# A 3x3 convolution on one core: the first output pair stored by halves, fewer loads issued ahead, idle matmuls four times as wide

## The chip, the cores and the metric

The kernel runs on one core of a Trainium2 chip. The core has TensorE (matrix products, its weight loads shown apart), VectorE, ScalarE, GpSimd and SyncE, each with an instruction queue of its own, and 16 DMA engines that all queues share. The metric is the device time of one execution in microseconds. The profile's span runs from the first to the last instruction; the time is a little longer.

## The reference

The input is 16 images of 64 channels, 64 by 64 pixels, in f32; the weight is 128 x 64 x 3 x 3, of which about nine in ten values are zero (the kernel does not use that). The output is 16 images of 128 channels:

```python
x_pad = np.pad(x, ((0, 0), (0, 0), (pad, pad), (pad, pad)), mode='constant')
for b in range(batch):
    for co in range(c_out):
        for ci in range(c_in):
            for kh in range(k):
                for kw in range(k):
                    if weight[co, ci, kh, kw] != 0:
                        output[b, co] += weight[co, ci, kh, kw] * x_pad[b, ci, kh:kh+h, kw:kw+w]
```

So 16.8 MB of input and 0.29 MB of weight are read, and 33.6 MB of output are written.

## The kernel before

Two images make a pair: 2 x 64 channels fill the 128 partitions, and there are eight pairs, 0 to 7. A pair's input is kept in a bf16 tile of its own, `xs[p]`; the f32 to bf16 conversion is done by the load itself, issued from GpSimd (`load`, L68). Only the first 32 rows of pair 0, the head, come as f32 through SyncE (L62), into the first buffer of the `o` pool, and are cast on VectorE and ScalarE (`cast_x`, L99). The `o` pool has seven buffers of one f32 output image each, so pair p uses two, and the buffers come round again after three pairs.

Every pair is worked off in four blocks of 16 rows, numbered here 0 to 31 through the whole kernel. Block 0 is computed directly (`direct`): nine taps per 8 rows and image. All others go through `twos`: GpSimd adds neighbouring rows (`s`, L167, in three buffers), TensorE makes one product of that sum for both output rows (copied out by ScalarE to `pc`, L174), then two products for the even and the odd rows (L148), and VectorE adds `pc` while it takes each out of PSUM (L181, four per block: even rows of image 0 and 1, then odd rows of image 0 and 1).

The order of each queue is the order of the program; nothing is rescheduled. SyncE issues the weight, the head, and then all stores: of pairs 0 to 6 one 2 MB store per image when the pair is done (L207), of pair 7 two of 1 MB per image, after its second and fourth block (L204). GpSimd issues the other half of pair 0 (L63), then pairs 1, 2 and 3 whole and 24 rows of pair 4 (L68). The other 40 rows of pair 4 are issued behind the sum of pair 1's last block, and pair p + 3 behind the sum of pair p's last block, for p = 2, 3, 4.

At the start, before any input is there, TensorE runs 27 matmuls on a tile of zeros (`keep_busy`, L84), which VectorE has cleared (L79); then nine that transpose the weights (L109); then 28 more on zeros. The first real matmul follows, and waits for the head's cast.

Of the kernel before, what the change touches and what calls it, by code (L numbers as in the profile page):

```python
# [8 lines left out]
FP32 = mybir.dt.float32  # L9
BF16 = mybir.dt.bfloat16  # L10
# [17 lines left out]
def kernel(  # L28
# [6 lines left out]
    nc = tc.nc  # L35

    B, C_IN, H, W = x.shape
    C_OUT, _, KH, KW = weight.shape
    assert (B, C_IN, H, W) == (16, 64, 64, 64) and (C_OUT, KH, KW) == (128, 3, 3)
    NP = B // 2  # L40
    HEAD = 32

    const_pool = ctx.enter_context(tc.tile_pool(name="const", bufs=1))
# [4 lines left out]
    psum_pool = ctx.enter_context(  # L48
        tc.tile_pool(name="psum", bufs=8, space=bass.MemoryType.PSUM)
    )  # L50
# [4 lines left out]
    def pair(p):  # L55
        return x[2 * p : 2 * p + 2].rearrange("n i h w -> (n i) h w")

    xs = [x_pool.tile([128, H, W], BF16, name=f"x{p}") for p in range(NP)]
# [5 lines left out]
    ident = const_pool.tile([128, 128], BF16, name="ident")  # L64
    make_identity(nc, ident)

    def load(p, a=0, b=H):
        nc.gpsimd.dma_start(out=xs[p][:, a:b, :], in_=pair(p)[:, a:b, :])  # L68

    EARLY, CUT = 4, 24
    for p in range(1, EARLY):
        load(p)
    load(EARLY, 0, CUT)


    idle_rhs = const_pool.tile([128, 128], BF16, name="idle_rhs")
    nc.vector.memset(idle_rhs, 0.0)  # L79
    idle_ps = psum_pool.tile([128, 128], FP32, name="ps")  # L80

    def keep_busy(n):
        for _ in range(n):
            nc.tensor.matmul(idle_ps, idle_rhs, idle_rhs, start=True, stop=True)  # L84

    keep_busy(27)

# [8 lines left out]
    def cast_x(copy, a, b):  # L98
        copy(out=xs[0][:, a:b, :], in_=x_head[:, a:b, :])  # L99
# [24 lines left out]
    nc.vector.tensor_copy(out=wT[:, G0], in_=ps0)  # L124
    ps2 = transposed(G2)
    nc.scalar.copy(out=wT[:, G2], in_=ps2)
    keep_busy(28)
    cast_x(nc.scalar.copy, 9, 18)
    difference(G01, ps0)
    difference(G21, ps2)  # L130
# [26 lines left out]
    def direct(p, o, r0, rows):  # L157
        ps = product(
            [(xs[p], G1, r0, 1), (xs[p], G0, r0 - 1, 1), (xs[p], G2, r0 + 1, 1)], rows
        )  # L160
        nc.scalar.copy(out=o[0][:, r0 : r0 + rows, :], in_=ps[0])  # L161
        nc.vector.tensor_copy(out=o[1][:, r0 : r0 + rows, :], in_=ps[1])  # L162

    def twos(p, o, r0):
        t0 = r0 // 2
        s = s_pool.tile([128, 8, W], BF16, name="s")
        nc.gpsimd.tensor_tensor(  # L167
            out=s, in0=xs[p][:, r0 : r0 + 16 : 2, :], in1=xs[p][:, r0 + 1 : r0 + 16 : 2, :], op=ADD
        )
        shared = product([(s, G1, 0, 1)], 8)  # L170
        pc = []
        for n in range(2):
            c = p_pool.tile([128, 8, W], FP32, name="pc")
            nc.scalar.copy(out=c, in_=shared[n])  # L174
            pc.append(c)
        even = [(xs[p], G21, r0 + 1, 2), (xs[p], G0, r0 - 1, 2)]
        odd = [(xs[p], G01, r0, 2), (xs[p], G2, r0 + 2, 2)]
        for first, terms in ((r0, even), (r0 + 1, odd)):
            ps = product(terms, 8)
            for n in range(2):  # L180
                nc.vector.tensor_tensor(  # L181
                    out=o[n][:, first : r0 + 16 : 2, :], in0=ps[n], in1=pc[n], op=ADD
                )

    for p in range(NP):
        o = [o_pool.tile([C_OUT, H, W], FP32, name="o") for _ in range(2)]
        last = p == NP - 1
        for blk in range(4):
            r0 = 16 * blk
            if BLOCKS[p][blk] == "T":  # L190
                twos(p, o, r0)


                if p == 1 and blk == 3:
                    load(EARLY, CUT, H)
                elif p > 1 and blk == 3 and p + EARLY - 1 < NP:
                    load(p + EARLY - 1)
            else:
                for r, rows in ((r0, 8), (r0 + 8, 8)):
                    direct(p, o, r, rows)  # L200
            if last and blk % 2 == 1:
                for n in range(2):
                    rows = slice(r0 - 16, r0 + 16)
                    nc.sync.dma_start(out=out[2 * p + n][:, rows, :], in_=o[n][:, rows, :])  # L204
        if not last:
            for n in range(2):
                nc.sync.dma_start(out=out[2 * p + n], in_=o[n])  # L207

# [29 lines left out]
```

## Time and profile before

| what | value |
|---|---|
| four runs, us | 126.51, 126.59, 131.04, 131.05 |
| their median, us | 128.81 |
| the profiled execution: time, us | 126.51 |
| its span, us | 124.7 |
| mean granted TensorE clock | 0.957 |
| busy share: TensorE, VectorE, GpSimd, ScalarE | 87%, 66%, 33%, 31% |
| matmuls of the computation (L148) | 966, from 7.23 us to about 110.3 us |
| VectorE's combinations (L181) | 124 of 686 ns |
| GpSimd's row sums (L167) | 31 of 1151 ns |
| loads with conversion (L68): issue to landing | 11.9 to 24.4 us |
| stores of 2 MB (L207): issue to landing | 10.3 to 25.6 us |
| stores of 1 MB (L204): issue to landing | 9.9 to 13.3 us |

Busy times are of one execution. In the lines on stretches of time the columns are: the stretch, its length, then busy time and number of instructions of TensorE, its weight loads, VectorE, ScalarE and GpSimd, then the granted TensorE clock, the DMA engines' share, and the GB/s that landed. In the lines of the timeline they are: start, length, engine, line of the kernel, operation, what is written from what, number of instructions, and in brackets the idle time before and what ended it. A DMA's landing is counted from its issue, so it holds the time that it stood behind other transfers.

### The profile page before, as it was taken

The page shows a single profiled execution, that of the slowest core. Times are in us where ns is not written, and L with a number is a line of the kernel's source. Part 1 is how long each engine was busy: PE and PEld are TensorE (multiplying, and loading weights), DVE is VectorE, ACT ScalarE, POOL GpSimd, SP SyncE. Part 2 cuts the span into 40 slices and gives each one's busy share as a digit, 9 for nine tenths or more (in the row PEclk, how much of TensorE's full clock was granted, in tenths as well). Part 3 has the DMA queues.
Part 4 walks back from the last instruction along what each step waited for, and adds up shares of the span by engine and source line. Part 5 has one row for each costly group of instructions (what it writes and reads, how often), then busy time and mean ns, then how long its engine had stood idle before and what let it go on. Part 6 is the DMA issues. An engine that isn't in the chain of part 4 may idle for free.

```text
span 124.7 us, 2543 instructions
## 1 busy us (share of the span) xinstructions
PE 108.9 (87%) x1030; PEld 59.8 (48%) x1030; DVE 82.3 (66%) x135; ACT 39.0 (31%) x71; POOL 41.1 (33%) x46
## 2 busy tenths in 40 slices
PE   6989999999999999999999999999999999940000
PEld 6845555555555555555555555555555555510000
DVE  0364777877787778777877787778777878870000
ACT  4555323333333333333333333333333333300000
POOL 6437343533353335333533333333333300000000
PEclk9999999999999999999999999999999999997555
DMA  4999999999999999999999999999999999999991
GB/s 134 345 227 215 213 215 213 203 386 334 339 428 410 310 297 331 439 305 331 313 433 315 299 334 418 420 439 420 436 436 420 431 426 426 431 407 420 428 389 50
DMA packets 4188, 42.93 MB, mean 344 GB/s; under 512 B 464, under 2 KB 464, under 8 KB 976
## 3 DMA queue, kind: packets, MB, share of 16 engines
q1 hardware_dynamic: 2880, 34.90, 66.6%
q0 software_dynamic: 1296, 7.86, 30.8%
q8 instruction: 8, 0.13, 0.4%
q14 instruction: 4, 0.03, 0.1%
HBM read 17.07 MB, written 33.55 MB: 406 GB/s over the span
## 4 chain that ended last, share of the span: by engine, by line
PE 82%; DMA 4%; DVE 1%; issue 1%; DVEq 0%; SPq 0%
PE ps L148 82%; DMA o<-in_x_dram 4%; DVE o L181 1%; DVEq L233 0%; DVE x L99 0%; SPq L60 0%; DVEq L181 0%
## 5 line engine op out<-in xcount | busy, mean ns | idle before, releaser
L181 DVE TENSOR_TENSOR o<-ps,pc 128x512 f32<-128x512 f32 x124 | 77.8, 686 | 22.1 <-PE ps L148 19.8
L148 PE MATMUL ps<-x,wT 64*128 64x504 bf16 (+3 forms) x780 | 88.8, 373 | 0.5 <-DVE x L99 0.5
L148 PEld LDWEIGHTS <-wT 64*128 64x128 bf16 x966 | 54.8, 94 | 48.8 <-issue 0.5
L167 POOL TENSOR_TENSOR s<-x 128x512 bf16<-128x512 bf16 x31 | 35.6, 1151 | 57.4 <-PE ps L148 43.2
L174 ACT COPY pc<-ps 128x512 f32<-128x512 f32 x62 | 33.3, 589 | 64.0 <-issue 61.8
L148 PE MATMUL ps<-s,wT 64*128 64x512 bf16 (+1 forms) x186 | 25.7, 377 | 0.0
L84 PE MATMUL ps<-idle_rhs 128*128 128x128 bf16 x55 | 4.8, 265 | 1.0 <-DVE idle_rhs L79 1.0
L84 PEld LDWEIGHTS <-idle_rhs 128*128 128x128 bf16 x55 | 4.4, 122 | 1.0 <-DVE idle_rhs L79 1.0
L68 POOL DMA_DIRECT2D x<-in_x_dram x8 | 4.4, 561 | 0.0
L103 DVE CAST w_bf<-w_sb 128x192 bf16<-128x192 f32 (+1 forms) x4 | 1.1, 360 | 2.6 <-DMA w_sb<-in_weight_dram 2.6
L162 DVE COPY o<-ps 128x512 f32<-128x512 f32 x2 | 1.4, 692 | 2.0 <-PE ps L148 2.0
L161 ACT COPY o<-ps 128x512 f32<-128x512 f32 x2 | 1.2, 586 | 2.4 <-PE ps L148 2.4
L99 ACT CAST x<-o 128x576 bf16<-128x576 f32 (+1 forms) x2 | 1.5, 803 | 1.1 <-DMA o<-in_x_dram 1.1
L99 DVE CAST x<-o 128x576 bf16<-128x576 f32 x1 | 0.5, 460 | 2.0 <-DMA o<-in_x_dram 2.0
L103 ACT ACT_TABLE_LOAD x1 | 1.3, 1283 | 0.7 <-PEq L222 0.7
L103 ACT CAST w_bf<-w_sb 128x64 bf16<-128x64 f32 (+1 forms) x2 | 0.7, 415 | 1.6 <-DMA w_sb<-in_weight_dram 1.6
L109 PE MATMUL ps<-ident,w_bf 128*128 128x128 bf16 x9 | 1.0, 265 | 0.1
L113 DVE TENSOR_TENSOR wT<-ps,wT 128x384 bf16<-128x384 f32 x2 | 1.0, 548 | 0.0
L63 POOL DMA_DIRECT2D x<-in_x_dram x1 | 0.7, 693 | 0.8 <-POOLq L222 0.8
L109 PEld LDWEIGHTS <-w_bf 128*128 128x128 bf16 x9 | 0.6, 112 | 0.5 <-DVE w_bf L103 0.5
L79 DVE MEMSET idle_rhs<- 128x64 uint32 x1 | 0.1, 112 | 0.8 <-PEq L222 0.8
L122 ACT CAST wT<-ps 128x384 bf16<-128x384 f32 x1 | 0.5, 479 | 0.4 <-PE ps L109 0.4
(8 smaller groups left out, 2.0 us busy)
## 6 DMA issues: line engine op xcount, KB each, us to landing
out_dram<-o SPq DMA_DIRECT2D x14, 2048.0 KB, 17.7
x<-in_x_dram POOLq DMA_DIRECT2D x6, 1024.0 KB, 15.9
out_dram<-o SPq DMA_DIRECT2D x4, 1024.0 KB, 11.6
o<-in_x_dram SPq DMA_DIRECT2D x1, 1024.0 KB, 5.5
x<-in_x_dram POOLq DMA_DIRECT2D x1, 640.0 KB, 14.1
x<-in_x_dram POOLq DMA_DIRECT2D x1, 512.0 KB, 7.6
x<-in_x_dram POOLq DMA_DIRECT2D x1, 384.0 KB, 24.4
w_sb<-in_weight_dram SPq DMA_DIRECT2D x1, 288.0 KB, 2.8
```

What stands on the lines that cost most here:

```text
L68: nc.gpsimd.dma_start(out=xs[p][:, a:b, :], in_=pair(p)[:, a:b, :])
L84: nc.tensor.matmul(idle_ps, idle_rhs, idle_rhs, start=True, stop=True)
L99: copy(out=xs[0][:, a:b, :], in_=x_head[:, a:b, :])
L103: copy(out=w_bf4[:, g, a:b, :], in_=w_v[:, k : k + b - a, :])
L109: nc.tensor.matmul(wps[:, j, :], src, ident, start=True, stop=True)
L113: nc.vector.tensor_tensor(out=wT[:, g], in0=wps, in1=wT[:, G1], op=SUB)
L148: nc.tensor.matmul(ps[n][:, lo:hi, c_lo:c_hi], tap(g, kw, n), src[q, a:b:step, c_lo + kw - 1 : c_hi + kw - 1], start=(i == 0), stop=(i == ...
L161: nc.scalar.copy(out=o[0][:, r0 : r0 + rows, :], in_=ps[0])
L162: nc.vector.tensor_copy(out=o[1][:, r0 : r0 + rows, :], in_=ps[1])
L167: nc.gpsimd.tensor_tensor(out=s, in0=xs[p][:, r0 : r0 + 16 : 2, :], in1=xs[p][:, r0 + 1 : r0 + 16 : 2, :], op=ADD)
L174: nc.scalar.copy(out=c, in_=shared[n])
L181: nc.vector.tensor_tensor(out=o[n][:, first : r0 + 16 : 2, :], in0=ps[n], in1=pc[n], op=ADD)
```

## The change

Three things change. The loads ahead are pair 1 and pair 2; pair 3 is issued behind the sum of block 5 (pair 1's second), pair 4 whole behind that of block 7, and pairs 5, 6 and 7 behind those of blocks 11, 15 and 19, where they were. Pair 0 is stored as pair 7 is, by halves after its second and its fourth block. And the matmuls on zeros are 128 by 512 instead of 128 by 128, seven and seven instead of 27 and 28, so that 7168 columns stand for 7040; the tile of zeros is four times as wide.

```diff
-    def load(p, a=0, b=H):
-        nc.gpsimd.dma_start(out=xs[p][:, a:b, :], in_=pair(p)[:, a:b, :])
-    EARLY, CUT = 4, 24
-    for p in range(1, EARLY):
+    def load(p):
+        nc.gpsimd.dma_start(out=xs[p], in_=pair(p))
+    for p in (1, 2):
         load(p)
-    load(EARLY, 0, CUT)
-    idle_rhs = const_pool.tile([128, 128], BF16, name="idle_rhs")
+    later = {5: 3, 7: 4, 11: 5, 15: 6, 19: 7}
+    idle_rhs = const_pool.tile([128, 512], BF16, name="idle_rhs")
     nc.vector.memset(idle_rhs, 0.0)
-    idle_ps = psum_pool.tile([128, 128], FP32, name="ps")
+    idle_ps = psum_pool.tile([128, 512], FP32, name="ps")
     def keep_busy(n):
         for _ in range(n):
-            nc.tensor.matmul(idle_ps, idle_rhs, idle_rhs, start=True, stop=True)
-    keep_busy(27)
+            nc.tensor.matmul(idle_ps, idle_rhs[:, 0:128], idle_rhs, start=True, stop=True)
+    keep_busy(7)
...
-    keep_busy(28)
+    keep_busy(7)
...
+    HALVES = (0, NP - 1)
     for p in range(NP):
         o = [o_pool.tile([C_OUT, H, W], FP32, name="o") for _ in range(2)]
-        last = p == NP - 1
         for blk in range(4):
             r0 = 16 * blk
             if BLOCKS[p][blk] == "T":
                 twos(p, o, r0)
-                if p == 1 and blk == 3:
-                    load(EARLY, CUT, H)
-                elif p > 1 and blk == 3 and p + EARLY - 1 < NP:
-                    load(p + EARLY - 1)
+                if 4 * p + blk in later:
+                    load(later[4 * p + blk])
             else:
                 for r, rows in ((r0, 8), (r0 + 8, 8)):
                     direct(p, o, r, rows)
-            if last and blk % 2 == 1:
+            if p in HALVES and blk % 2 == 1:
                 for n in range(2):
                     rows = slice(r0 - 16, r0 + 16)
                     nc.sync.dma_start(out=out[2 * p + n][:, rows, :], in_=o[n][:, rows, :])
-        if not last:
+        if p not in HALVES:
             for n in range(2):
                 nc.sync.dma_start(out=out[2 * p + n], in_=o[n])
```

## The prediction

> **What bounds the kernel now.** I read the chain of waits first, then the 40 slices, then busy time by stretches, and last the opening in order of time. The chain in order of time (start, length, what) is nearly one piece:
>
> ```profile
> 1.16 5.53 DMA o<-in_x_dram
> ...
> 6.71 0.47 DVE x L99
> ...
> 7.23 102.09 PE ps L148 x954
> ...
> 111.27 0.60 DVE o L181
> ```
>
> It reads as a TensorE bound, but it stops at 111.87 of 124.7 us. What follows is stores, and the slices show that they were late long before:
>
> ```profile
> DMA  4999999999999999999999999999999999999991
> ...
> HBM read 17.07 MB, written 33.55 MB: 406 GB/s over the span
> ```
>
> In the stretches (the last two columns are the DMA share and what landed, GB/s) the 16 engines never pause after the first bytes:
>
> ```profile
> 0.00:2.00 2.00, 1.01 (x10) 1.01 (x11) 0.11 (x1) 1.27 (x1) 0.97 (x6) 1.00 0.12 18
> 2.00:6.00 4.00, 3.92 (x48) 3.46 (x46) 1.14 (x4) 1.71 (x5) 2.54 (x6) 1.00 1.01 351
> 6.00:17.60 11.60, 11.06 (x111) 6.11 (x110) 6.86 (x12) 4.83 (x8) 5.63 (x5) 1.00 1.05 218
> 17.60:24.00 6.40, 6.40 (x64) 3.44 (x62) 5.08 (x9) 2.15 (x4) 2.83 (x3) 1.00 1.02 201
> 24.00:37.00 13.00, 13.00 (x126) 6.93 (x122) 10.22 (x18) 4.30 (x8) 5.11 (x5) 1.00 1.03 359
> 37.00:62.00 25.00, 25.00 (x238) 13.29 (x234) 19.46 (x32) 8.60 (x16) 10.22 (x10) 1.00 1.02 345
> 62.00:85.00 23.00, 23.00 (x219) 12.22 (x216) 18.06 (x30) 7.52 (x14) 8.06 (x7) 1.00 1.01 381
> 85.00:120.00 35.00, 25.51 (x240) 13.32 (x236) 21.33 (x35) 8.60 (x16) 5.77 (x5) 0.91 1.00 426
> ```
>
> What lands is counted. A load reads f32 and lands bf16, half the bytes, so 218 landed in 6 to 17.6 us is 436 GB/s read, beside 426 GB/s for stores alone after 85 us. The engines run from about 1.76 us (share 0.24 in the second microsecond) to about 121.6 (0.58 in 121 to 122): 119.8 us for 17.07 + 33.55 = 50.62 MB. That is the bound. TensorE has slack at the end: the last two 1.05 MB stores are issued at 111.6 to 111.9 and alone need 2.1 / 0.426 = 4.9 us, so with 1 us from issue to first byte they could be done by 117.8; the engines go on to 121.6, so 3.8 us are older work. Nothing helps that does not shorten the engines' 119.8 us or move its two ends; what opens a gap in them adds to the time.
>
> **The change, part by part.** The profiled execution took 126.51 us, 1.81 more than its span. Of the four runs two lie there (126.51, 126.59) and two at 131.04 and 131.05, so the median, 128.81, is a time that no run had. I sum against 126.51; the profile does not tell what the other two spent.
>
> *Bytes.* The same tensors move, 50.62 MB: no term.
>
> *When the loads run out.* Pair 3 (2.10 MB read) and 24 rows of pair 4 (0.79) leave the opening. What remains lands as 0.295 (weights) + 1.049 (head, f32) + 0.524 + 2 x 1.049 = 3.97 MB. By 6.0 us 0.04 + 4 x 0.351 = 1.44 MB have landed; the other 2.53 at 218 GB/s take 11.6 us, to 17.6 us. There the engines would idle, unless stores are ready.
>
> *When the first stores come.* Now they leave SP after the third L181 of block 3, 1.98 us after that block's first L181 (19.73 to 21.71 below). Block 1's first is at 13.25, so the half store of `o[0]` goes at 15.23, `o[1]`'s some 0.7 us later.
>
> ```profile
> 8.31 3.37 POOL L167 TENSOR_TENSOR s<-x 128x512 bf16<-128x512 bf16 x3 [3.69 <-ACT x L99]
> ...
> 13.25 2.51 DVE L181 TENSOR_TENSOR o<-ps,pc 128x512 f32<-128x512 f32 x4 [1.30 <-PE ps L148]
> ...
> 14.55 2.26 POOL L167 TENSOR_TENSOR s<-x 128x512 bf16<-128x512 bf16 x2 [2.86 <-PE ps L148]
> ...
> 18.51 1.16 POOL L167 TENSOR_TENSOR s<-x 128x512 bf16<-128x512 bf16 x1 [1.70 <-PE ps L148]
> 19.73 2.48 DVE L181 TENSOR_TENSOR o<-ps,pc 128x512 f32<-128x512 f32 x4 [0.73 <-PE ps L148]
> ...
> 21.71 0.88 SPq L207 DMA_DIRECT2D out_dram<-o  x2
> ```
>
> From issue to first byte the weight load took 1.0 us (0.74 to 1.76): stores flow from 16.2, a cover of 1.4 us. The upper bound is the store issued at 21.71: what landed rises above the loads' level only in 24 to 25 us (292 GB/s), up to 3.3 us later, which would leave 15.23 + 3.3 - 17.6 = 0.9 us of idle engines. But at 21.71 loads still held the engines, so that delay is mostly queueing. I take 0, and 0 to 0.9 for the range; a gain is excluded, since the engines were not idle here.
>
> *The next hand-overs.* Pair 3 is issued behind the sixth `s` (POOL free at 16.81). At 17.6 most of a 2.1 MB half pair and 2.1 MB of load are outstanding: 4.2 / 0.43 = 9.8 us, to 27.4. Second halves (21.71) and pair 4 (22.8, where now 40 of its rows go) add 9.8 us, to 37.2. Pair 1's stores go at 34.45, cover 37.2 - 35.45 = 1.7 us. By then both kernels have issued the same bytes, and later issues stand at the same places.
>
> *POOL.* Of its loads, two of about 0.55 us leave the opening, before a 3.69 us wait. The moved one, 0.57 us, lands in the 1.70 us of idleness ahead of `s` at 18.51; pair 4's replaces one issue by one. No term.
>
> *Data.* Loads took 11.9 to 24.4 us to land. Pair 3 comes by 28.7 to 41.2 us; TensorE wants its first sum at 46.3 (a block each 3.2 us from 11.03, the 12th), POOL 1.15 us sooner, at 45.1: cover 3.9 us at worst. Pair 4 issued at 22.8 lands by 47.2 at worst, and is wanted near 58.
>
> *SP and buffers.* SP issues two DMAs more, some 0.35 us each, and it idles between stores. Stores share eight completion counters, so each waits also for the DMA eight issues earlier on SP; that is now at latest pair 4's store (issued by 74, landed within 18.6) before the last half at 111. VectorE's first write into pair 3's `o[1]` waits for both halves of pair 0's first image: issued by 21.7, landed 13.1 us later in this trace, wanted after 46.
>
> *Store shape.* Four 1.05 MB stores replace two of 2.10. Whole stores (84 to 100 us) landed 428 GB/s, the stretch with the last pair's halves (100 to 120) 422: 4.19 / 0.422 - 4.19 / 0.428 = +0.14 us. I take it; ends are -0.1 and +0.3, as such windows scatter by that. The Trainium skill, "DMA: Bandwidth & Descriptors", section "Bandwidth", speaks against halves: a lone 1 MB transfer reached 341 GB/s, 16 MB reached 425. By it the first pair would take 4.19 / 0.341 - 4.19 / 0.425 = 2.4 us more, an estimate of 129.0 us; the 422 here was reached with other work outstanding.
>
> *Mixing.* 2.88 MB of loads move from alone (436) to among stores. In 24 to 85 us 13 x 0.359 + 25 x 0.345 + 23 x 0.381 = 22.1 MB landed; some 4.1 MB were loads (pairs 5 to 7, pair 4's rest, about 0.3 left over), so 26.2 MB moved, 429 GB/s. 2.88 / 0.429 - 2.88 / 0.436 = +0.1, and as much back where stores then run with fewer loads: 0, within 0.2.
>
> *Idle matmuls.* 27 took 3.06 us, a step of (3.06 - 0.27) / 26 = 107 ns per 128 columns; 28 took 1.73 us, 54 ns: the clock had come up by 4.96, though the granted clock reads 1.00 throughout. Seven wide steps are 7 x 4 x 107 = 3.0 us, then 7 x 4 x 54 = 1.5 us. The memset writes four times as much, 0.112 to at most 0.45 us, so transposes start 0 to 0.2 us after 4.13. The second batch then ends by 6.9, and real matmuls wait for the head's cast until 7.23 (0.54 us idle). No term; if the cover were gone, 0.2 us.
>
> Sum: 126.51 + 0.14 = 126.65; with the unknown costs, 126.2 to 127.9.
>
> **The rivals.** *Slower: the clock comes up late.* Seven wide matmuls on zeros do not keep it up, or not in time. If the second batch stays slow it ends at 4.96 + 3.0 = 7.96, 0.73 us late; if the first block's 3.99 us of matmuls do too, the delay is 4.7 us. Stores then flow at 20.9 with loads run out at 17.6 (POOL's next load waits for the same matmuls): 3.3 us of idle engines, 130.0 us. It decides from 1.4 us of delay on, and costs over 2% from 4.0. Against it: as many busy columns in both batches. The skill's "TensorE: Matmul & The Clock Gate", Part 1, makes it about 3.4 us of sustained activity, in windows not tied to the kernel's start, and not a number of matmuls; one window more (to 8.4 us) would by that give an estimated 0.9 us of delay, inside the cover. Chance 0.13.
>
> *Faster: the engines run better* because stores and loads overlap from 16 us. At 436 GB/s in place of 429 up to 37 us it gives 35.2 x 7 / 436 = 0.6 us, 126.0; over 2% would need 124.0, that is 431 GB/s on the whole instead of 422. One stretch (75 to 80 us) had 434, but the mixed ones show nothing above 429. Chance 0.07.
>
> *The early stores do not do what they say:* they come after the loads ran out, and 0.9 us are lost, 127.5. Chance 0.08.
>
> **How the numbers follow.** My forecast, no change, has 0.72: 126.6 us, own range 125.9 to 127.6. About 2% is what a measurement of this kernel can tell from no change. Faster by more 0.07 (the second rival in its strong form), slower by more 0.13 (the first), within 0.80 (forecast and third). The range reaches from 125.6 up to 131.2, which takes in the first rival's 130.0 and the 131.05 that the unchanged code also shows, plus 0.14.
>
> **What would show it.** Landed GB/s near 213 until about 16 us, then rising; a DMA share near 1 in every microsecond from 2 to 121; the half stores at about 15.2 and 15.9 on SP; the second idle batch at 54 ns per 128 columns; real matmuls from 7.2 to 110; a span of 124.5 to 125.5. Wrong: a DMA share under 0.9 at 17 to 19 or 35 to 38 us, matmuls starting late, or VectorE waiting on a DMA at the start of a pair.

## The result, and the profile after

The changed kernel takes 126.99 us in the median of all 43 runs, the kernel before 126.53 us in the median of all 64. The ratio is 1.004, with a 95% interval of 1.0027 to 1.0053: about 0.5 us slower, well under 2% but clear of the scatter. (A few executions of either kernel take 128.4 to 132.5 us; the ratios leave those out, and so do the spreads and the experiments' medians below.) The profiled execution of the changed kernel took 126.7 us, its span is 124.9. The runs of the changed kernel also lie less close together: of before nearly all are within 126.3 and 127.2, of the changed kernel they reach from 126.4 to 128.3.

The chain of waits in order of time (start, length, what) now begins on TensorE, and the first real matmul comes at 7.52 in place of 7.23 us:

```profile
1.19 3.17 PE ps L84 x7
4.36 1.05 PE ps L109 x9
5.41 2.10 PE ps L84 x7
7.52 102.04 PE ps L148 x954
```

The second batch of wide matmuls took 2.1 us of the chain, where seven at the faster step would take 1.5. That is visible, and it is not the cause, as the first two experiments show. The same stretches as before (last two columns: DMA share, GB/s landed):

```profile
6.00:17.60 11.60, 11.60 (x102) 5.12 (x102) 6.63 (x12) 4.83 (x8) 6.20 (x6) 1.00 1.05 215
17.60:24.00 6.40, 6.40 (x64) 2.96 (x62) 5.08 (x9) 2.15 (x4) 2.81 (x3) 1.00 1.01 349
24.00:37.00 13.00, 13.00 (x126) 5.96 (x122) 10.22 (x17) 4.29 (x8) 5.11 (x5) 1.00 1.01 275
37.00:62.00 25.00, 25.00 (x238) 11.42 (x234) 19.46 (x32) 8.59 (x16) 10.23 (x10) 1.00 1.03 349
...
85.00:120.00 35.00, 25.73 (x242) 11.57 (x238) 21.57 (x35) 8.59 (x16) 5.77 (x5) 0.94 1.00 427
```

The change did what it says: stores land from about 18 us (349 GB/s landed instead of 201), loads from 24 to 37 us (275 instead of 359). And the engines' share is 1.0 throughout, so no idle engine is to be seen. To see the loss one has to count what the engines moved, not how long they were busy. The DMA queues' lines give packets, MB landed and share, each packet counted where it starts; q0 carries the converting loads, whose bytes read are twice those landed, q1 the stores. For 17 to 27 us, before and then after:

```profile
q0 software_dynamic: 320, 1.59, 81.5%
q1 hardware_dynamic: 56, 0.92, 21.7%
```

```profile
q1 hardware_dynamic: 293, 2.15, 53.4%
q0 software_dynamic: 130, 0.93, 47.8%
```

Moved: 2 x 1.59 + 0.92 = 4.10 MB before, 2 x 0.93 + 2.15 = 4.01 after. From 27 to 37 us, again before and then after:

```profile
q1 hardware_dynamic: 193, 2.90, 69.0%
q0 software_dynamic: 146, 0.66, 32.1%
```

```profile
q0 software_dynamic: 188, 1.31, 63.9%
q1 hardware_dynamic: 203, 1.52, 37.2%
```

that is 4.22 and 4.14 MB. In these 20 us the changed kernel falls behind by 0.17 MB, 0.4 us at 0.43 MB per us, with busy engines. The count of bytes, summed from the start over such windows, is the view by which I read the runs below, numbered e1 to e17 (MB moved by the end of each time):

| kernel | 17 us | 27 us | 37 us | 62 us | 88 us | 118 us |
|---|---|---|---|---|---|---|
| before | 6.30 | 10.40 | 14.62 | 25.27 | 36.36 | 49.09 |
| after | 6.28 | 10.31 | 14.45 | 25.21 | 36.19 | 49.01 |
| wide idle matmuls alone (e1) | 6.25 | 10.49 | 14.64 | 25.30 | 36.45 | 49.18 |
| early halves of pair 0 alone (e3) | 6.27 | 10.14 | 14.38 | 25.10 | 36.18 | 48.88 |
| fewer loads ahead alone (e4) | 6.27 | 9.79 | 13.89 | 24.52 | 35.66 | 48.38 |
| halves of pair 0 at its end (e10) | 6.30 | 10.41 | 14.63 | 25.29 | 36.39 | 49.07 |
| halves of pair 2 (e13) | 6.28 | 10.39 | 14.61 | 25.06 | 36.12 | 48.89 |
| halves of pair 6 (e12) | 6.27 | 10.44 | 14.64 | 25.32 | 36.39 | 49.09 |

Single sums scatter by some 0.1 MB, which is the size of the difference at 118 us between before and after in these two executions (0.08 MB, 0.2 us, as their times differ); the steps of 0.2 MB and more are what is read from it. So the two steps of the changed kernel, 0.09 and 0.08 MB, do not show by themselves where it loses: at 62 us it is 0.06 MB behind. The experiments with larger steps have to show that.

### The profile page after: what moved, and what is told of

The parts are those of the page before. It is cut to its first block, busy times and chain, and to the rows that moved or that the text cites. A ratio compares the mean times of both kernels' runs of the same rounds, so it can differ in the third digit from the quotient of the medians.

```text
span 124.9 us, 2466 instructions
## 1 busy us (share of the span) xinstructions
PE 109.5 (88%) x989; PEld 49.6 (40%) x989; DVE 82.4 (66%) x135; ACT 38.9 (31%) x71; POOL 40.6 (33%) x45
## 4 chain that ended last, share of the span: by engine, by line
PE 87%; DVE 1%; issue 1%; DVEq 0%
PE ps L148 82%; PE ps L84 4%; DVE o L181 1%; PE ps L109 1%; DVEq L233 0%; DVE idle_rhs L79 0%; DVEq L181 0%
## 5 line engine op out<-in xcount | busy, mean ns | idle before, releaser
L148 PEld LDWEIGHTS <-wT 64*128 64x128 bf16 x966 | 47.1, 94 | 56.2 <-issue 0.4
L148 PE MATMUL ps<-s,wT 64*128 64x512 bf16 (+1 forms) x186 | 25.2, 377 | 0.0
L84 PE MATMUL ps<-idle_rhs 128*128 128x512 bf16 x14 | 5.5, 557 | 1.2 <-DVE idle_rhs L79 1.2
L68 POOL DMA_DIRECT2D x<-in_x_dram x7 | 3.9, 564 | 0.0
L84 PEld LDWEIGHTS <-idle_rhs 128*128 128x128 bf16 x14 | 1.7, 134 | 3.6 <-issue 2.2
L63 POOL DMA_DIRECT2D x<-in_x_dram x1 | 0.7, 693 | 0.8 <-POOLq L222 0.8
```

The costliest lines, as they stand in the source:

```text
L68: nc.gpsimd.dma_start(out=xs[p], in_=pair(p))
L84: nc.tensor.matmul(idle_ps, idle_rhs[:, 0:128], idle_rhs, start=True, stop=True)
L148: nc.tensor.matmul(ps[n][:, lo:hi, c_lo:c_hi], tap(g, kw, n), src[q, a:b:step, c_lo + kw - 1 : c_hi + kw - 1], start=(i == 0), stop=(i == ...
```

## The experiments

**The three parts of the change, each alone or left out.** First the 14 wide matmuls alone:

```diff
 # kernel before
-    idle_rhs = const_pool.tile([128, 128], BF16, name="idle_rhs")
+    idle_rhs = const_pool.tile([128, 512], BF16, name="idle_rhs")
...
-    idle_ps = psum_pool.tile([128, 128], FP32, name="ps")
+    idle_ps = psum_pool.tile([128, 512], FP32, name="ps")
...
-            nc.tensor.matmul(idle_ps, idle_rhs, idle_rhs, start=True, stop=True)
+            nc.tensor.matmul(idle_ps, idle_rhs[:, 0:128], idle_rhs, start=True, stop=True)
-    keep_busy(27)
+    keep_busy(7)
...
-    keep_busy(28)
+    keep_busy(7)
```

> The kernel before with the 14 wide idle matmuls alone (7168 columns for 7040); loads and stores as before. The changed kernel measured 1.004, and its runs spread from 126.4 to 128.4 us where those of before lie within 126.3 to 127.2. Theory A (opening): the wide matmuls bring the clock up later, in some runs by more than in others (the second batch took 2.31 us against 1.73), real matmuls start late and the DMA engines run dry; then this kernel shows all of it: 1.003 to 1.005, with the same spread and the first real matmul 0.2 to 2 us later. Theory B (loads and stores): 1.000, no spread. Theory C (a late start costs only where the loads run out earlier): 1.000 to 1.002 here, although the first real matmul is late.

Measured (e1): 126.57 us, ratio 1.0008 (0.9987 to 1.003). In its profiled execution, too, the first real matmul is late:

```profile
7.53 1.82 PE L148 MATMUL ps<-x,wT 64*128 64x512 bf16 x16 [0.65 <-DVE x L99]
```

But here the second batch took 1.73 us, as in the kernel before, and the matmul waits for the head, whose cast began at 7.01 instead of 6.71 us; in the changed kernel's trace it waited for a batch of 2.1 us with the same matmuls. So the slow batch does not come in every execution. Over all runs the wide matmuls alone cost nothing that this measures; theory A expected 1.003 to 1.005. The complement, the changed kernel with the narrow matmuls, decides it:

```diff
 # changed kernel
-    idle_rhs = const_pool.tile([128, 512], BF16, name="idle_rhs")
+    idle_rhs = const_pool.tile([128, 128], BF16, name="idle_rhs")
...
-    idle_ps = psum_pool.tile([128, 512], FP32, name="ps")
+    idle_ps = psum_pool.tile([128, 128], FP32, name="ps")
...
-            nc.tensor.matmul(idle_ps, idle_rhs[:, 0:128], idle_rhs, start=True, stop=True)
+            nc.tensor.matmul(idle_ps, idle_rhs, idle_rhs, start=True, stop=True)
-    keep_busy(7)
+    keep_busy(27)
...
-    keep_busy(7)
+    keep_busy(28)
```

> The changed kernel with the 27 and 28 narrow idle matmuls of before; its loads and stores stay. A: 1.000, spread as before. B: 1.004 with the spread of the changed kernel. C: 1.000 to 1.001, since the start is on time again.

Measured (e2): 127.07 us, 1.0044 (1.0022 to 1.0067), with runs from 126.5 to 127.9. The whole cost remains without the wide matmuls, so it is in the loads and stores, and theory A falls. A spread of over 1 us remains as well; the wide matmuls alone spread too, though less (eight of ten runs within 126.3 to 126.7, two at 127.2 and 127.5). Of the loads and stores, the halves alone:

```diff
 # kernel before
-        last = p == NP - 1
+        last = p in (0, NP - 1)
```

> The kernel before with the first pair stored by halves, loads ahead as before (three pairs and 24 rows of pair 4). The prediction priced the smaller stores at +0.14 us (1.001). A and C: 1.000 to 1.001. B: up to 1.004 if it is the smaller stores or the stores mixing with the loads; 1.000 if it is the loads.

Measured (e3): 126.90 us, 1.0032 (1.0019 to 1.0046), runs from 126.74 to 127.18. By 27 us its row in the table is 0.26 MB behind that of before. And the loads alone:

```diff
 # changed kernel, narrow idle matmuls
-    HALVES = (0, NP - 1)
+    HALVES = (NP - 1,)
```

> The kernel before with fewer loads ahead (two pairs; pair 3 behind block 5's sum, pair 4 whole behind block 7's) and the first pair stored whole at 21.7 us. By the prediction's bound the loads run out at 17.6, pair 3's load (2.1 MB, 4.9 us at 430 GB/s, first bytes near 18) carries the engines to about 22.9 and the first stores flow at 22.7: 0.4 to 1 us of idle engines, 127.0 to 127.6 us (1.004 to 1.008). If TensorE were what ends last instead, 1.000.

Measured (e4): 127.98 us, 1.0101 (1.0072 to 1.013). Here the loss is one of idle or ill-fed engines, and its stretches show it (last two columns: share, GB/s landed):

```profile
16.00:17.00 1.00, 1.00 (x14) 0.41 (x11) 0.31 (x1) 0.74 (x2) 1.00 (x2) 1.00 1.05 221
17.00:18.00 1.00, 1.00 (x12) 0.47 (x10) 0.96 (x2) 0.00 (x0) 0.65 (x2) 1.00 0.72 147
18.00:19.00 1.00, 1.00 (x14) 0.46 (x10) 1.00 (x3) 0.04 (x1) 0.00 (x0) 1.00 1.34 123
19.00:20.00 1.00, 1.00 (x12) 0.42 (x10) 0.55 (x1) 1.00 (x2) 0.93 (x1) 1.00 0.68 66
20.00:21.00 1.00, 1.00 (x12) 0.49 (x10) 0.72 (x2) 0.03 (x1) 0.22 (x1) 1.00 0.83 172
```

The loads run out at 17 to 18 us, as worked out; pair 3's load, issued at 17.08, lands at close to the full rate only from 21 us (205 GB/s landed). By 27 us 0.61 MB are missing against before (9.79 for 10.40), 1.4 us, and the time is 1.5 us longer. So a gap in the DMA engines' work does reach the end, and TensorE's slack does not absorb it. In the whole change the early stores fill this gap (377 GB/s landed from 18 to 19 us): halves and fewer loads each cost alone, and together (1.0044 in e2) they cost little more than the halves do (1.0032).

**Shape or time of the halves.** A first attempt issued all four halves in order behind the pair's last block:

```diff
 # kernel before
-        if not last:
+        if not last and p == 0:
+            for half in range(2):
+                for n in range(2):
+                    rows = slice(32 * half, 32 * half + 32)
+                    nc.sync.dma_start(out=out[2 * p + n][:, rows, :], in_=o[n][:, rows, :])
+        elif not last:
```

> The kernel before with pair 0's stores cut into four of 1 MB, but all four issued after its last block, as before: the shape of the early halves without their time. Halves alone, issued early, gave 1.0032 and a narrow spread (126.74 to 127.18). Theory S (shape: two DMAs and 288 packets more cost the engines' time): 1.003 again. Theory M (it is the early stores that run beside the opening's loads): 1.000.

Measured (e5): 126.91 us, 1.0034 (1.0022 to 1.0045). It does not tell what it was made for: SyncE waits only for the rows that a store reads, and nothing stood before it in its queue, so the first halves went when block 1 was done. The trace has store packets from 19 us on, as with early halves. It is a repetition of those. The first halves of each pair go early also in the kernel that cuts pairs 0 to 6 (`p == 0` replaced by `p >= 0`):

> The kernel before with the stores of pairs 0 to 6 all cut into halves and all issued at their pair's end: 14 DMAs more where the first pair alone has two. Theory S: seven times 0.3 to 0.4 us, 128.6 to 129.3 us (1.017 to 1.022). Theory M: 1.000, 126.4 to 126.7.

Measured (e6): 128.31 us, 1.0142 (1.0128 to 1.0155): 14 DMAs more cost 1.8 us. SyncE waited 8.3 us in it for earlier stores (the eight counters), which the kernels before it do not show, so its price per pair is not a clean one. With the second half put first in the queue all four stores wait for the last block:

```diff
 # kernel before
+        if p == 0:
+            for half in (1, 0):
+                for n in range(2):
+                    rows = slice(32 * half, 32 * half + 32)
+                    nc.sync.dma_start(out=out[2 * p + n][:, rows, :], in_=o[n][:, rows, :])
-        if not last:
+        elif not last:
```

> The kernel before with pair 0's stores in halves, the second half first in the queue, so that all four wait for the pair's last block. (In the earlier run meant as late halves the queue let the first halves go when their own rows were done, near 15.5 us; it was the early halves once more.) P: 1.003, 126.9 us. M: 1.000, 126.5 us.

Measured (e10): 126.58 us, 1.0003 (0.9992 to 1.0013). The two additional DMAs and 288 additional packets cost nothing that this measures. What costs is that the halves are issued earlier, among the opening's loads. Theories S and P fall. These late halves had a load beside them, too, the 40 rows of pair 4. From 27 to 37 us they moved the same bytes as the whole stores of before (their lines for this window stand in the section on the result):

```profile
q1 hardware_dynamic: 401, 2.90, 70.9%
q0 software_dynamic: 144, 0.66, 32.1%
```

So halves beside a load do not lower the rate in every case.

**Whether the hand-over from loads to stores had too little cover.** The changed kernel with 24 rows of pair 3 loaded ahead:

```diff
 # changed kernel
-    def load(p):
-        nc.gpsimd.dma_start(out=xs[p], in_=pair(p))
+    def load(p, a=0, b=H):
+        nc.gpsimd.dma_start(out=xs[p][:, a:b, :], in_=pair(p)[:, a:b, :])
...
     for p in (1, 2):
         load(p)
+    load(3, 0, 24)
...
-                    load(later[4 * p + blk])
+                    load(later[4 * p + blk], 24 if later[4 * p + blk] == 3 else 0)
```

> The changed kernel with 24 rows of pair 3 loaded ahead as well (0.79 MB, 1.8 us of the engines) and the other 40 behind block 5's sum; all else as in the changed kernel, wide idle matmuls too. Theory G (loads run out just as the early stores' first bytes come, 2.3 to 2.5 us after their issue, so that the cover is nil and some runs have a gap of 0 to 2 us): the spread up to 128.4 us goes, all runs within 0.8 us of each other. With S or M on top the median is 126.8 to 127.0; without them 126.5. If the spread stays, G falls.

Measured (e7): 127.53 us, 1.0081 (1.0068 to 1.0094), runs from 127.44 to 127.65. The spread went, as G expected, but the time rose by 0.5 us over the changed kernel's, which G did not expect. The 24 rows were alone on the engines from 18 to 20 us; here is their line, and then the line of before for the same window, in which whole rows move:

```profile
q0 software_dynamic: 88, 0.25, 96.1%
```

```profile
q0 software_dynamic: 58, 0.43, 102.0%
```

At nearly the same share 88 packets landed 0.25 MB instead of 0.43 MB by 58: 250 GB/s read. Not all of that is the size of the rows: the kernel before reads the 24 rows of pair 4, alone from 23 to 24 us, at 320 GB/s (0.16 MB landed). With a whole pair 3 ahead instead:

```diff
 # changed kernel
-    for p in (1, 2):
+    for p in (1, 2, 3):
...
-    later = {5: 3, 7: 4, 11: 5, 15: 6, 19: 7}
+    later = {7: 4, 11: 5, 15: 6, 19: 7}
```

> The changed kernel with pair 3 loaded whole ahead instead of behind block 5's sum: the loads ahead last to about 22.5 us, the first stores' bytes come near 18, every load is in one piece. P with G (a hand-over without cover): no spread, 126.4 to 126.6 (1.000), since the halves' cost is paid back by pair 4 in one piece. M: 126.9 to 127.1 (1.003 to 1.005).

Measured (e9): 126.81 us, 1.0043 (1.0019 to 1.0067): six runs at 126.6 to 126.8 and five at 127.3 to 128.1, so that the median lies lower than the ratio suggests. With a cover of several us the spread stays and the cost shows no difference: G falls as the cause of both. Two more, on loads in pieces:

```diff
 # kernel before (e8)
-    load(EARLY, 0, CUT)
+    load(EARLY)
...
-                if p == 1 and blk == 3:
-                    load(EARLY, CUT, H)
-                elif p > 1 and blk == 3 and p + EARLY - 1 < NP:
+                if p > 1 and blk == 3 and p + EARLY - 1 < NP:
```

> The kernel before with pair 4 loaded whole ahead (four whole pairs ahead, no pair in two pieces), stores as before. Theory P (transfers in pieces cost the engines' time: two packets of a partition's row instead of one; a load in 24 and 40 rows as well as a store in halves): 0.3 to 0.5 us less, 126.0 to 126.2 (0.996 to 0.998). Theory M (early stores beside loads cost): 1.000.

```diff
 # kernel before (e11)
-                    load(p + EARLY - 1)
+                    load(p + EARLY - 1, 0, CUT)
+                    load(p + EARLY - 1, CUT, H)
```

> The kernel before with the loads of pairs 5, 6 and 7 each issued in two pieces, 24 and 40 rows, one right behind the other: three DMAs more, as pair 4 has them. P: 0.3 to 0.5 us for each, 127.4 to 128.0 (1.007 to 1.012). M: 1.000.

Four whole pairs ahead (e8): 127.05 us, 1.0043 (1.0029 to 1.0057), the opposite of what P said, and M did not expect it either. Its stores are whole and were issued from 22.02 us, but moved no byte before 26 us, while the loads went on. From 24 to 26 us these loads, whole rows and alone on the engines, landed

```profile
q0 software_dynamic: 36, 0.29, 101.9%
```

that is 290 GB/s read instead of 430. From 20 to 27 us this kernel moved 2.66 MB and before 2.80. So in its opening bytes are lost, at a full share, where whole stores enter beside a whole load; how much of the 0.5 us this makes was not followed further. Three more loads in pieces (e11): 126.54 us, 1.0002 (0.9979 to 1.0025), runs from 126.1 to 127.3. Those pieces, beside other work, cost nothing that this measures.

**Halves beside loads, and halves beside none.** In each, one other pair gets the halves, its stores being issued when their rows are done:

```diff
 # kernel before
-        last = p == NP - 1
+        last = p in (6, NP - 1)    # e12; (2, NP - 1) in e13
```

> The kernel before with pair 6's stores in halves, each issued when its rows are done; no load is left by then. Theory Q (half rows of stores alternating with whole rows of loads lower the engines' rate): 1.000. Theory E (an earlier half store costs wherever it stands): 1.003.

> The kernel before with pair 2's stores in halves, which run beside the loads of pairs 5 and 6. Q: some 8 us beside loads at 413 instead of 430 GB/s, 0.3 us, 126.8 us (1.002 to 1.003). E: 1.003 as well; with 1.000 both fall, and the cost belongs to the place where the stores first enter among the opening's loads.

Pair 6, where no load is left (e12): 126.47 us, 0.9999 (0.998 to 1.0019). Pair 2, beside the loads of pairs 5 and 6 (e13): 126.90 us, 1.0033 (1.0005 to 1.006), runs from 126.6 to 127.8. Theory E falls. The queues' lines from 50 to 62 us, before and then with pair 2's halves:

```profile
q1 hardware_dynamic: 207, 3.05, 60.3%
q0 software_dynamic: 133, 1.03, 41.0%
```

```profile
q1 hardware_dynamic: 303, 2.79, 55.8%
q0 software_dynamic: 152, 1.05, 43.3%
```

3.05 + 2 x 1.03 = 5.11 MB against 2.79 + 2 x 1.05 = 4.89: 0.22 MB, 0.5 us (give or take the 0.1 MB by which such sums scatter; this execution was 0.3 us longer than that of before), at shares of 101% and 99%. In the table above the row of this kernel agrees with before up to 37 us and falls behind by 62; the row of pair 6 never does. Where pair 6's halves are on the engines, 100 to 112 us, before and then with them:

```profile
q1 hardware_dynamic: 357, 5.05, 99.0%
```

```profile
q1 hardware_dynamic: 636, 5.00, 99.1%
```

nearly twice the packets carry the same bytes in the same time.

**Whether it is the size of the rows that alternate.** Four runs were to tell whether the engines lose because an 8 KB row of a store takes its turn beside a 16 KB row of a load.

```diff
 # changed kernel (e14; load takes a range of rows, as in e7)
-                    load(later[4 * p + blk])
+                    q = later[4 * p + blk]
+                    if q in (3, 4):
+                        load(q, 0, 32)
+                        load(q, 32, H)
+                    else:
+                        load(q)
```

> The changed kernel with pairs 3 and 4 each loaded as two halves of 32 rows, issued one right behind the other at the places of the whole loads, so that a load's row is 8 KB read beside a half store's 8 KB. Q: the rate beside loads rises to that of equal packets, 126.5 to 126.7 us (1.000 to 1.001). E, or the place of the entry: 1.004 as the changed kernel.

```diff
 # kernel before (e15 with P = 0, e16 with P = 6)
+            if p == P:
+                for n in range(2):
+                    rows = slice(r0, r0 + 16)
+                    nc.sync.dma_start(out=out[2 * p + n][:, rows, :], in_=o[n][:, rows, :])
...
-        if not last:
+        if not last and p != P:
```

> The kernel before with pair 0 stored by quarters, 16 rows (4 KB of a partition) after each block. Q (the smaller a store's rows against a load's whole rows beside them, the lower the engines' rate): more than the halves' 1.0033, 1.005 to 1.010. If only the early entry beside loads matters, whatever the size: 1.003 to 1.004.

> The kernel before with pair 6 stored by quarters, no loads beside them: the control for the quarters' own cost. Q: 1.000 to 1.001. If small rows cost by themselves: 1.003 or more.

```diff
 # kernel before (e17)
-    EARLY, CUT = 4, 24
-    for p in range(1, EARLY):
+    EARLY, CUT = 4, 32
+    for p in range(1, EARLY - 1):
         load(p)
+    load(EARLY - 1, 0, CUT)
+    load(EARLY - 1, CUT, H)
     load(EARLY, 0, CUT)
...
-        last = p == NP - 1
+        last = p in (0, NP - 1)
```

> The kernel before with early half stores of pair 0, and pair 3's opening load as well as pair 4's loads in halves of 32 rows (8 KB read for 8 KB stored). Q: 1.000 to 1.001, against 1.0032 and 1.0034 with a whole pair 3 and with 24 and 40 rows of pair 4. If the sizes do not matter: 1.003.

Equal halves in the changed kernel (e14): 126.94 us, 1.0029 (1.0006 to 1.0051). Quarters in pair 0 (e15): 127.52 us, 1.0073 (1.0056 to 1.0089). Quarters in pair 6 (e16): 126.88 us, 1.0032 (1.0021 to 1.0043). Early halves with equal halves of loads (e17): 126.94 us, 1.0024 (1.0004 to 1.0045). Quarters in pair 0 cost about twice what the halves cost, as Q expected, but quarters also cost 0.3% where no load is beside them, which Q did not. In that control SyncE waited for earlier stores, 7.6 us in all, and in the run with pair 0 it did not, so the one cannot simply be taken off the other. Equal sizes bring a gain that no interval separates from none. So the size of the rows as the cause is neither shown nor excluded.

What is shown is the condition: half stores issued early, while loads run. That their alternating with loads lowers the rate throughout is not shown, and the trace of e3 speaks against it. From 27 to 37 us it has halves beside loads in

```profile
q1 hardware_dynamic: 328, 2.42, 59.2%
q0 software_dynamic: 243, 0.91, 44.8%
```

2 x 0.91 + 2.42 = 4.24 MB, where before moved 4.22. What it lost, it lost earlier: it moved 1.15 MB instead of 1.30 from 17 to 20 us, where its first store bytes come (at 19.2), and 1.08 instead of 1.26 from 24 to 27 (e5, the repetition: 1.11 and 1.04); between these it was slightly ahead, 1.62 to 1.54. Together with e8, where whole stores lose bytes as they enter beside a whole load, this leaves a rival that no run here separates: that what costs is the entry of the stores among running loads, and not their shape. The loss in pair 2, where stores had long entered, speaks against it as the only cause, but that interval begins at 1.0005.

## Why the prediction was wrong

No change was forecast, at 126.65 us against the profiled 126.51, and the kernel is 0.5 us slower.

**The bound was right.** The DMA engines set the end. With fewer loads ahead alone they ran dry at 17 to 18 us, and the time grew by 1.5 us (e4). A later start of TensorE, by 0.3 us in the profiled execution of e1, shows no cost there (1.0008, up to 1.003), which fits its 3.8 us of slack. The expectation for e4 put its gap at 0.4 to 1 us; it was larger, for the reason of the next point but one.

**The step that failed is the mixing term,** "0, within 0.2". I took the rate of loads among stores, 429 GB/s, from stretches in which every store was a whole 2 MB image; I took the price of half stores from the end of the kernel, where no load runs, and added the two as if they were independent. What no row of before shows is half stores issued early among the opening's loads. They cost 1.0032 and 1.0034 by themselves (e3, e5), 0.4 us, while the same halves issued behind the pair's last block measure 1.0003 (e10) and early halves without loads 0.9999 (e12). That is nearly the size of the measured 1.0040, which also stays with the narrow matmuls (1.0044) and with a third pair loaded ahead (1.0043). It is not a sum of prices: fewer loads ahead cost 1.0101 alone, and the early stores fill most of that gap. Of the signs of being wrong that the prediction named, matmuls starting late showed and had no price, and a DMA share under 0.9 at 17 to 19 us did not show (0.95 to 1.00): the loss is in the bytes. For the +0.14 us of the store shape nothing is measured in e10 and e12, but their intervals reach to 1.0013 and 1.0019 and do not exclude it.

**The first stores' bytes came 2 to 4 us after their issue, not 1.0.** In the changed kernel the first half store is issued at 15.49, and q1 moves nothing until 17.7 us. The prediction's cover of 1.4 us was in truth nothing; the bound that it kept, 0 to 0.9 us of idle engines (its third rival), allows for that. In e4 the first whole store, issued at 22.26, moved its first bytes at 24.3. But with plenty of cover (e9) the cost is 1.0043 as well, so this is not what cost.

**The first rival, a late clock,** happened in the profiled execution and had no price: the second wide batch took 2.1 us of the chain, the first real matmul came 0.3 us late, the wide matmuls alone measure 1.0008, and without them the cost stays (1.0044). The 1.4 us of delay from which the prediction let it count was not reached. **The second rival** has nothing for it.

**The chance for within 2% was right, the range's own reason was not.** The measured median lies in the range and in the forecast's own range, but that is in part luck: the range was spread for a slower rival that did not come, and the sum lacked the 0.4 us that did.

**Still open:** why the engines move fewer bytes at a share of 1.0 when half stores are issued early beside loads, and whether their shape or their entry does it; and what spreads the runs of the changed kernel and of e1, e2, e9, e11, e13 and e14 over 1 to 2 us, when those of e3, e5, e7, e8, e10, e15, e16 and e17 lie within 0.7 us.

No version tried beats the kernel before.

## What to carry to other kernels

When DMA engines are the bound, a busy share of 1.0 does not mean that bytes move at the full rate: sum what the queues moved over the same windows in both profiles, and the place of a loss of half a microsecond shows. A price for a transfer's shape holds for the neighbours it was measured with; half stores cost nothing measurable in e10 and e12, and 0.4 us a pair when they were issued early beside converting loads. And an order of issue that is meant to delay a store does so only if something ahead of it in the queue waits, since a store waits for its own rows alone.

## What the runs showed of the hardware that was not expected

Early halves of stores (8 KB of a partition) beside whole converting loads: 408 GB/s moved over 12 us in e13 (4.89 MB), where whole stores beside the same loads moved 426 (5.11 MB), with the share at 99% and 101%; in one execution each, and not in every stretch, since from 27 to 37 us the kernels with halves beside a load, e3 and e10, moved as much as before with whole stores (4.24, 4.22 and 4.22 MB). A converting load of 24 rows alone on the engines read 250 GB/s (e7, 18 to 20 us) and 320 (before, 23 to 24 us) where whole rows read 430. And no store byte moved before 26 us when four whole loads stood ahead of stores issued at 22.02 us (e8), 4 us later, while in the last 2 us of these the load, alone, read only 290 GB/s.
